# Three score products for a tile instead of four in a chunked gated recurrence (HGRN2) on one core

## The chip, the cores and the metric

The kernel runs on one core of one Trainium2 chip. A core has a matrix engine (PE, with a weight load, PEld, that can run beside the matmuls), a vector engine (DVE), a scalar engine (ACT), a general engine (POOL) and DMA queues, which the kernel issues from SP for the most part. The metric is the device time of one execution in microseconds (us); lower is better. Several executions are timed and the median is given.

## The reference

One layer of a hybrid trunk is computed: adaLN, an HGRN2 gated linear recurrence in both directions over 2048 latent tokens with a prefix of 256 context tokens, an output product, then a gated ConvFFN and a last RMSNorm. The change lies in the recurrence. For each of 8 heads and each direction, with a decay f per token and per key channel, k = 1 - f, and b the running sum of log f:

```python
def hgrn2_chunk_scan(q, k, v, logf, s0):
    """S_t = diag(f_t) S_{t-1} + k_t v_t^T, o_t = S_t^T q_t, in chunkwise form."""
    b = jnp.cumsum(logf, axis=3)
    b_ref = b[:, :, :, CHUNK // 2:CHUNK // 2 + 1]
    b_last = b[:, :, :, -1:]
    qe = q * jnp.exp(b - b_ref)
    ke = k * jnp.exp(b_ref - b)
    scores = jnp.einsum('bhnik,bhnjk->bhnij', qe, ke)
    scores = jnp.where(mask, scores, 0.0)          # causal
    o_intra = jnp.einsum('bhnij,bhnjv->bhniv', scores, v)
    kv = jnp.einsum('bhnjk,bhnjv->bhnkv', k * jnp.exp(b_last - b), v)
    ...                                            # the state S is carried from chunk to chunk
    o_inter = jnp.einsum('bhnik,bhnkv->bhniv', q * jnp.exp(b), s_start)
    o = o_intra + o_inter
```

So a pair (query i, key j) of one chunk has the score q_i . k_j weighted in every channel by the product of the decays between j and i. The forward direction takes j up to i, the backward direction j from i on, and the outputs of both are added.

## The kernel before

**Tiles and units.** The 18 tiles of 128 tokens (two of context, 16 of latents) are taken in two groups of three "units" of three tiles (`GROUPS`). For each group, the loop goes over the 8 heads, and for each head over the three units: 48 calls of `unit`, of which the 8 with the context have one latent tile and 40 have three, so 128 latent tiles times heads in all. A tile of 128 tokens is cut into four segments of 32; a unit has 12 segments (`NS`).

**What a unit does.** Products with the weights go through `mm3` (lines 358 to 360: three fp32r products stand for one of fp32). `unit` first makes the decays of two directions (`d` 0 is the backward one here and `d` 1 the forward one, whose tokens are read in reverse order, line 390), then q and the values v. On DVE it scans the decays within each segment (`S`, line 436, from the segment's far side; then over `F` in the other direction, line 449), forms the keys `ke` (lines 441, 442), the reciprocals `rt` of each segment's total decay (line 451) and the queries `qp` (lines 455, 456). POOL makes from the segment totals the small tables `TB` (decays before and after a segment within its tile) and `TX` (lines 464 to 475). The helper `scaled` (line 480) multiplies a whole operand by one factor per segment: it makes `kd` (keys for the state), `qe` (queries times `rt`), `qi` (queries for the state), and `qm` and `km` (queries and keys for pairs whose segments lie in different halves of the tile). ACT copies `kx`, keys of alternating directions (lines 505, 506).

**What a tile does.** Each tile has a `part_a` and a `part_b`, returned as a list and run during the next unit, between that unit's products (`fill` hands them out). `part_a` transposes `kd` on PE (line 530, evicted by ACT at 532), and makes four products into one PSUM tile `sc` (lines 538, 539, 544, 545): own segment backward, own segment forward, neighbour segment within a half, and across the halves. ACT copies two 64x64 blocks of the fourth (lines 549, 550), DVE copies three more under masks `mx`, `mb`, `mf` (lines 551 to 553) and adds the two halves `af` and `ab` into the score tile `at` (line 554). `part_b` makes the state increment `kv` (line 562), the outputs `o` from the state `Sf` and from `at` (lines 577, 578), evicts them and updates `Sf` (line 581). What the pass over the other direction needs is stored in `stash`.

**What sets the order.** The order in which each engine gets its instructions is not the order of the text: a planner places them by the dependencies between tiles and its own estimate of their times. Tiles of one tag share a fixed number of buffers (`kd` one, `ke`, `qp`, `kx`, `sc` two). After the recurrence come the output product and the ConvFFN, which the change does not touch.

Of the kernel before, what the change touches and what calls it, by code (L numbers as in the profile page):

```python
# [9 lines left out]
F32 = mybir.dt.float32  # L10
F32R = mybir.dt.float32r
BF16 = mybir.dt.bfloat16
U32 = mybir.dt.uint32
# [9 lines left out]
NH = 8  # L23
# [25 lines left out]
def body(ctx, tc, a, out):  # L49
# [123 lines left out]
    def load_feat(h, **kw):  # L173


        feat = []
        for ty in (2, 1):
            wh = wp.tile([128, KT, 128], F32R, name="wh", tag="wh")
            wl = wp.tile([128, KT, 128], F32R, name="wl", tag="wl")
            load_w(h, ty, wh, wl, **kw)  # L180
            feat.append((wh, wl))
        vh = wp.tile([128, KT, 384], F32R, name="vh", tag="vh", bufs=1)
        vl = wp.tile([128, KT, 384], F32R, name="vl", tag="vl", bufs=1)
        load_w(h, 0, vh[:, :, 256:], vl[:, :, 256:], **kw)
        return feat, vh, vl
# [101 lines left out]
    def mixer_scan():  # L287
# [13 lines left out]
        def mask(name):  # L301
            m = fix.tile([128, 4, 32], F32, name=name)
            pool.memset(m, 1.0)
            return m

        mf, mb, mx = mask("mf"), mask("mb"), mask("mx")
        in_block(mb, 32)
        in_block(mx.rearrange("p (a c) b -> p a (c b)", c=2), 64)
        dve.tensor_tensor(mx, mx, mb, OP.subtract)
        in_block(mf, 32)  # L310
        for m, s in ((mf, 1), (mb, -1)):
# [3 lines left out]
        mfu, mbu, mxu = [m.rearrange("p a b -> p (a b)").bitcast(U32) for m in (mf, mb, mx)]  # L315
        d1 = fix.tile([128, NS, SEG], BF16, name="d1")
# [5 lines left out]
        TBs = [fix.tile([128, 4, NSC, 4], F32, name=f"TB{i}") for i in range(2)]  # L322
        TXs = [fix.tile([128, 2, NSC, 4], F32, name=f"TX{i}") for i in range(2)]
        for i in range(2):
            pool.memset(Fs[i], 1.0)
            pool.memset(TBs[i], 1.0)
            pool.memset(TXs[i], 1.0)
            for d in range(2):
                pool.memset(ABs[i][d], 0.0)
# [32 lines left out]
        def unit(h, w, u, tiles, todo):  # L362
# [23 lines left out]
            for d in range(2):  # L386
                z = ps.tile([128, UN], F32, name="z", tag="pj", bufs=3)
                mm3(z, *feat[d], vh, vl)
                zv = z.rearrange("p (c t) -> p c t", t=32)
                act.activation(F[:, d, :, 1:SEG], zv[:, :, 31::-1] if d else zv, AF.Sigmoid)  # L390
                j = (1 - d) * NH + h
                dve.tensor_scalar(F[:, d, :, 1:SEG], F[:, d, :, 1:SEG],
                                  oml[:, j:j + 1], lb[:, j:j + 1], OP.mult, OP.add)
                fill(1 + d)
# [40 lines left out]
            for d in range(2):  # L435
# [4 lines left out]
            ke = gp.tile([128, 2, NS, 32], F32, name="ke", tag="ke", bufs=2)  # L440
            dve.tensor_tensor(ke[:, 0], S[:, 0, :, 0:32], S[:, 0, :, 1:SEG], OP.subtract)
            dve.tensor_tensor(ke[:, 1, :, 31::-1], S[:, 1, :, 0:32], S[:, 1, :, 1:SEG],
                              OP.subtract)


# [6 lines left out]

            qp = gp.tile([128, 2, NS, 32], F32, name="qp", tag="qp", bufs=2)
            qv = q.rearrange("p (c t) -> p c t", t=32)
            dve.tensor_tensor(qp[:, 0, lat], qv, F[:, 0, lat, 1:SEG], OP.mult)
            dve.tensor_tensor(qp[:, 1, lat], qv, F[:, 1, lat, 32:0:-1], OP.mult)

# [12 lines left out]
            pool.tensor_tensor(suf[:, :, :, 0], suf[:, :, :, 1], tot[:, :, :, 1], OP.mult)  # L470
            pool.tensor_copy(decb[:, h, tiles[s0]:tiles[-1] + 1], sd[:, 0, s0:])
            pool.tensor_copy(TX[:, 0, :, 0], tot[:, 0, :, 1])  # L472
            pool.tensor_copy(TX[:, 0, :, 3], tot[:, 1, :, 2])
            pool.tensor_copy(TX[:, 1, :, 0], tot[:, 1, :, 1])
            pool.tensor_copy(TX[:, 1, :, 3], tot[:, 0, :, 2])

            def scaled(dst, src, w):

                w = w[..., None].to_broadcast(list(w.shape) + [32])
                dve.tensor_tensor(dst, src, w, OP.mult)  # L480
# [6 lines left out]
            kd = gp.tile([128, 2, NS, 32], F32, name="kd", tag="kd")  # L487
            scaled(kd, ke, TBf[:, 0:4:3])


            qe = gp.tile([128, 2, NS, 32], F32, name="qe", tag="qe", bufs=2)
            scaled(qe[:, :, lat], qp[:, :, lat], rt[:, :, lat])
            qi = gp.tile([128, 2, NS, 32], F32, name="qi", tag="qi", bufs=2)
            scaled(qi[:, :, lat], qp[:, :, lat], TBf[:, 1:3, lat])


            qm = gp.tile([128, NSC, 4, 32], F32, name="qm", tag="qm", bufs=2)
            km = gp.tile([128, NSC, 4, 32], F32, name="km", tag="km", bufs=2)
            scaled(qm[:, s0:, 0:2], seg(qp[:, 0])[:, :, 0:2], TX[:, 0, s0:, 0:2])
            scaled(qm[:, s0:, 2:4], seg(qp[:, 1])[:, :, 2:4], TX[:, 0, s0:, 2:4])  # L500
            scaled(km[:, s0:, 0:2], seg(ke[:, 1])[:, :, 0:2], TX[:, 1, s0:, 0:2])
            scaled(km[:, s0:, 2:4], seg(ke[:, 0])[:, :, 2:4], TX[:, 1, s0:, 2:4])

            kx = gp.tile([128, NS, 32], F32, name="kx", tag="kx", bufs=2)
            act.activation(kx[:, g0::2], ke[:, 1, g0::2], AF.Copy)
            act.activation(kx[:, g0 + 1::2], ke[:, 0, g0 + 1::2], AF.Copy)

# [18 lines left out]
            def part_a(s):  # L526
# [7 lines left out]
                if s < s0:  # L534
                    return

                sc = ps.tile([128, 4, 128], F32, name="sc", tag="sc", bufs=2)
                pe.matmul(sc[:, 0], ke[:, 0, g4], qe[:, 0, g4], start=True, stop=True)
                pe.matmul(sc[:, 1], ke[:, 1, g4], qe[:, 1, g4], start=True, stop=True)

                c0 = qp[:, 0, 4 * s]
                qx = bass.AP(tensor=c0.tensor, offset=c0.offset,
                             ap=[list(c0.ap[0]), [64, 2], [(NS + 1) * 32, 2], [1, 32]])
                pe.matmul(sc[:, 2], kx[:, g4], qx, start=True, stop=True)
                pe.matmul(sc[:, 3], km[:, s], qm[:, s], start=True, stop=True)
# [4 lines left out]
                act.activation(af[64:128, 0:64], sc[64:128, 3, 0:64], AF.Copy)  # L550
                dve.copy_predicated(af, mxu, sc[:, 2])
                dve.copy_predicated(af, mbu, sc[:, 0])
                dve.copy_predicated(ab, mfu, sc[:, 1])
                dve.tensor_tensor(at, af, ab, OP.add)
                ats[s] = at

            def part_b(s):
# [5 lines left out]
                if s < s0:  # L563
                    kb = gp.tile([128, 3, 128], F32, name="kb", tag="st", bufs=4)
                    act.activation(kb[:, 0], kv[:, 0], AF.Copy)
                    kvb.append(kb[:, 0])
                    if s == 0:
                        dve.tensor_copy(Sf[:, h], kv[:, 1])
                    else:
                        dve.scalar_tensor_tensor(Sf[:, h], Sf[:, h], sd[:, 1, s:s + 1], kv[:, 1],  # L570
                                                 OP.mult, OP.add)
                        dve.scalar_tensor_tensor(Sb[:, h], kvb[1], sd[:, 0, 0:1], kvb[0],
                                                 OP.mult, OP.add)
                    return
                st = sts[s]
                o = ps.tile([128, 128], F32, name="o", tag="o")
                pe.matmul(o, qi[:, 1, g4], Sf[:, h], start=True, stop=False)
                pe.matmul(o, ats[s], v[:, s], start=False, stop=True)
                act.activation(st[:, 0], o, AF.Copy)
                act.activation(st[:, 2], kv[:, 0], AF.Copy)  # L580
                dve.scalar_tensor_tensor(Sf[:, h], Sf[:, h], sd[:, 1, s:s + 1], kv[:, 1],
                                         OP.mult, OP.add)
                t = tiles[s]
                if is_late(h, t):
                    pool.tensor_copy(st[:, 3], qi[:, 0, g4].rearrange("p g t -> p (g t)"))
                    return
# [3 lines left out]
                q_.dma_start(stash[t][:, 0, h, 0], st[:, 2])  # L590
                sp.dma_start(stash[t][:, 0, h, 1], qi[:, 0, g4].rearrange("p g t -> p (g t)"))

# [818 lines left out]
```

## Time and profile before

| what | value |
|---|---|
| time before, median of 3 runs | 2908.31 us (2906.58 to 2913.72) |
| profiled execution: span from first to last instruction | 2911.0 us |
| profiled execution: time around the span | not recorded apart from the span |
| PE busy | 2841.6 us (98%) |
| DVE busy | 2120.3 us (73%) |
| ACT busy | 1168.5 us (40%) |
| POOL busy | 588.7 us (20%) |
| the recurrence | from about 80 to 1370 us of the span |
| mean granted clock of PE | 0.990 |

The profile is of one execution; its span is 2.7 us above the median of the three timed runs. A busy time is the union of an engine's instructions: matmuls overlap in the pipeline, so the duration of one matmul is longer than its share of the engine's time, and the distance from one start to the next is what a matmul costs. An fp32 product of 128 columns is recorded as two matmuls (two passes); an fp32r product is recorded as one.

### The profile page before, as it was taken

What the parts mean: (1) busy time and instruction counts of PE and PEld (TensorE: products, weight loads), DVE (VectorE), ACT (ScalarE), POOL (GpSimd) and SP (SyncE); (2) the same over time, 40 slices, a digit from 0 to 9 for tenths busy, and PEclk for the clock granted to TensorE, in tenths of its full rate; (3) what the DMA queues carried; (4) which work ended last, traced back from release to release, by engine and by line L of the source; (5) the groups of instructions that cost most, each with busy time, mean ns of one, the idle gap of its engine ahead of it and who ended that gap; (6) DMA issues with size and microseconds to landing.
All of it is one profiled execution on the core that took longest, in us unless ns stands there. A gap on an engine that the chain in (4) does not pass through costs nothing.

```text
span 2911.0 us, 44065 instructions
## 1 busy us (share of the span) xinstructions
PE 2841.6 (98%) x16192; PEld 2564.3 (88%) x16192; DVE 2120.3 (73%) x3676; ACT 1168.5 (40%) x2496; POOL 588.7 (20%) x1028
## 2 busy tenths in 40 slices
PE   8899999999999999998999799999999999999999
PEld 8899999998999999998888688888888888887887
DVE  1666666667666667667898498888798887677887
ACT  1533333336333333333455444444444444433343
POOL 1111111111111111111111254434443342000001
PEclk9999999999999999999999899999999999999999
DMA  5022222223222222224677722223622224887663
GB/s 217 25 89 79 80 86 84 77 67 107 81 72 79 77 80 89 70 80 140 237 289 291 307 87 87 87 87 110 238 87 87 87 80 129 271 297 246 204 204 119
DMA packets 202913, 386.57 MB, mean 133 GB/s; under 512 B 26693, under 2 KB 117829, under 8 KB 197449
## 3 DMA queue, kind: packets, MB, share of 16 engines
q1 hardware_dynamic: 199960, 375.51, 38.4%
q10 hardware_dynamic: 2736, 8.26, 0.8%
q8 instruction: 127, 2.08, 0.3%
q14 instruction: 90, 0.73, 0.1%
HBM read 281.70 MB, written 101.99 MB: 132 GB/s over the span
## 4 chain that ended last, share of the span: by engine, by line
PE 90%; DVE 3%; DMA 2%; ACT 2%; issue 1%; POOL 1%; SPq 0%; DVEq 0%; POOLq 0%; ACTq 0%
PE z L360 10%; PE z L359 10%; PE z L358 10%; PE y L1245 4%; PE y L1243 4%; PE y L1244 4%; PE zd L720 3%; PE zc L720 3%; PE zc L722 3%; PE zd L722 3%; PE zd L723 3%; PE zc L723 3%; PE za L720 3%; PE za L722 3%; PE za L723 3%; PE y L804 2%
## 5 line engine op out<-in xcount | busy, mean ns | idle before, releaser
L358 PE MATMUL z<-vh,hh 128*128 128x256 f32 (+1 forms) x1024 | 300.0, 293 | 0.0
L360 PE MATMUL z<-vh,hl 128*128 128x256 f32 (+1 forms) x1024 | 293.5, 287 | 0.0
L359 PE MATMUL z<-vl,hh 128*128 128x256 f32 (+1 forms) x1024 | 293.4, 287 | 0.0
L358 PE MATMUL z<-hh,wh 128*128 128x384 f32 x768 | 263.7, 344 | 9.6 <-ACT hh L80 9.6
L359 PE MATMUL z<-hl,wh 128*128 128x384 f32 x768 | 259.8, 338 | 0.6 <-DVE hl L81 0.5
L360 PE MATMUL z<-hh,wl 128*128 128x384 f32 x768 | 259.8, 338 | 0.0
L1245 PE MATMUL y<-wd,ml 128*128 128x512 f32 x600 | 234.5, 391 | 2.2 <-DVE ml L81 2.1
L1243 PE MATMUL y<-wd,mh 128*128 128x512 f32 x600 | 234.3, 390 | 1.8 <-ACT X L1278 1.8
L1244 PE MATMUL y<-wd,mh 128*128 128x512 f32 x600 | 234.0, 390 | 0.0
L358 PEld LDWEIGHTS z<-vh,hh 128*128 128x128 f32 x1024 | 196.4, 192 | 0.0
L359 PEld LDWEIGHTS z<-vl,hh 128*128 128x128 f32 x1024 | 196.2, 192 | 0.0
L360 PEld LDWEIGHTS z<-vh,hl 128*128 128x128 f32 x1024 | 195.8, 191 | 0.0
L81 DVE TENSOR_TENSOR w<-s,w 128x512 fp32r<-128x512 f32 x132 | 145.6, 1110 | 50.8 <-ACT w L80 50.5
L472 POOL COPY TX<-S 128x3 f32<-128x3 f32 x48 | 15.8, 330 | 775.2 <-DVE S L436 775.2
L81 DVE TENSOR_TENSOR w<-raw,w 128x512 fp32r<-128x512 f32 x176 | 132.2, 754 | 40.2 <-ACT w L80 39.6
L358 PEld LDWEIGHTS z<-hh,wh 128*128 128x128 f32 x768 | 145.6, 190 | 13.6 <-ACT hh L80 10.1
L412 DVE TENSOR_TENSOR st<-z,st 128x128 f32<-128x128 f32 x127 | 36.6, 288 | 157.4 <-ACT st L411 157.3
L1007 DVE SCALAR_TENSOR_TENSOR r<-uv,conv,r 128x1023 f32<-128x1023 f32 (+1 forms) x88 | 150.5, 1728 | 0.4
L80 ACT ACTIVATE w<-raw 128x512 fp32r<-128x512 f32 x176 | 109.0, 627 | 103.3 <-DMA raw<-in_w_up_dram 34.6
L359 PEld LDWEIGHTS z<-hl,wh 128*128 128x128 f32 x768 | 145.8, 190 | 1.3 <-DVE hl L81 1.3
L407 ACT ACTIVATE v<-z 128x128 f32<-128x128 f32 x128 | 35.4, 277 | 275.1 <-PE z L360 275.0
L360 PEld LDWEIGHTS z<-hh,wl 128*128 128x128 f32 x768 | 145.5, 189 | 0.0
(323 smaller groups left out, 8246.8 us busy)
## 6 DMA issues: line engine op xcount, KB each, us to landing
raw<-in_w_up_dram SPq DMA_DIRECT2D x90, 512.0 KB, 3.4
raw<-in_w_in_dram SPq DMA_DIRECT2D x80, 512.0 KB, 3.4
lr<-m SPq DMA_DIRECT2D x49, 512.0 KB, 5.6
m<-r SPq DMA_DIRECT2D x66, 256.0 KB, 3.3
raw<-in_w_ada_dram SPq DMA_DIRECT2D x32, 512.0 KB, 4.5
stash<-st SPq DMA_DIRECT2D x125, 128.0 KB, 1.9
kq<-stash SPq DMA_DIRECT2D x15, 1024.0 KB, 7.4
og<-stash SPq DMA_DIRECT2D x15, 1024.0 KB, 6.9
```

Of the source, the lines that this page charges most:

```text
L80: act.activation(h, src, AF.Copy)
L81: dve.tensor_tensor(l, src, h.bitcast(F32), OP.subtract)
L358: pe.matmul(o, sh[:, k], mh[:, k], start=k == 0, stop=False)
L359: pe.matmul(o, sh[:, k], ml[:, k], start=False, stop=False)
L360: pe.matmul(o, sl[:, k], mh[:, k], start=False, stop=k == KT - 1)
L720: pe.matmul(o, w[:, 0, k], r[:, :, 0, k], start=start and k == 0, stop=False, skip_group_check=True)
L722: pe.matmul(o, w[:, 0, k], r[:, :, 1, k], start=False, stop=False, skip_group_check=True)
L723: pe.matmul(o, w[:, 1, k], r[:, :, 0, k], start=False, stop=k == 3, skip_group_check=True)
L1007: dve.scalar_tensor_tensor(r, x, cw, r, OP.mult, OP.add)
L1243: pe.matmul(z, lh, rh, start=start, stop=False, skip_group_check=True)
L1244: pe.matmul(z, lh, rl, start=False, stop=False, skip_group_check=True)
L1245: pe.matmul(z, ll, rh, start=False, stop=stop, skip_group_check=True)
```

## The change

Keys and queries get different weights from before, so that three products hold all pairs of a tile. Direction 0 becomes the forward one and direction 1 the backward one. For segments taken alternately, either the keys or the queries are multiplied in place by `rt`: the keys `ke` of odd segments in direction 0 and of even segments in direction 1, and the queries `qp` of the other parity. The separate operands `qe`, `qm` and `km` are gone. A third plane of `qp`, called `far`, holds the queries for the other half of the tile. The first product takes `kx` against the scaled queries, the second and third take `ke` of one direction against unscaled queries of alternate segments and `far`. Their PSUM tile has three parts instead of four. Two masks and two masked copies take the place of three; the second goes to two blocks of columns at once. `kx` is copied by one ACT instruction instead of two. `TX` has one table instead of two, made by two copies and two products instead of four copies. The masks are built once, at the start, by another list of POOL instructions.

```diff
-        for ty in (2, 1):
+        for ty in (1, 2):
...
-        mf, mb, mx = mask("mf"), mask("mb"), mask("mx")
...
+        mx, my, mw = mask("mx"), mask("my"), mask("mw")
+        in_block(mx, 32)
+        pool.tensor_copy(mw, mx)
+        causal(mx, False)
+        causal(mw, True)
+        pool.tensor_copy(mx[:, 1::2], mw[:, 1::2])
+        pool.memset(mw, 1.0)
+        in_block(mw.rearrange("p (a c) b -> p a (c b)", c=2), 64)
+        pool.tensor_copy(by_two(my)[:, 0], by_two(mw)[:, 0])
+        pool.tensor_copy(by_two(my)[:, 1], by_two(mw)[:, 1])
...
-                act.activation(F[:, d, :, 1:SEG], zv[:, :, 31::-1] if d else zv, AF.Sigmoid)
-                j = (1 - d) * NH + h
+                act.activation(F[:, d, :, 1:SEG], zv if d else zv[:, :, 31::-1], AF.Sigmoid)
+                j = d * NH + h
...
-            qp = gp.tile([128, 2, NS, 32], F32, name="qp", tag="qp", bufs=2)
+            qp = gp.tile([128, 3, NS, 32], F32, name="qp", tag="qp", bufs=2)
...
-            pool.tensor_copy(TX[:, 0, :, 0], tot[:, 0, :, 1])
-            pool.tensor_copy(TX[:, 0, :, 3], tot[:, 1, :, 2])
-            pool.tensor_copy(TX[:, 1, :, 0], tot[:, 1, :, 1])
-            pool.tensor_copy(TX[:, 1, :, 3], tot[:, 0, :, 2])
+            pool.tensor_copy(TX[:, :, 1], tot[:, 0, :, 1])
+            pool.tensor_copy(TX[:, :, 2], tot[:, 1, :, 2])
+            pool.tensor_tensor(TX[:, :, 0], tot[:, 1, :, 1], tot[:, 1, :, 2], OP.mult)
+            pool.tensor_tensor(TX[:, :, 3], tot[:, 0, :, 1], tot[:, 0, :, 2], OP.mult)
...
-            scaled(kd, ke, TBf[:, 0:4:3])
-            qe = gp.tile([128, 2, NS, 32], F32, name="qe", tag="qe", bufs=2)
-            scaled(qe[:, :, lat], qp[:, :, lat], rt[:, :, lat])
+            scaled(kd, ke, TBf[:, 1:3])
             qi = gp.tile([128, 2, NS, 32], F32, name="qi", tag="qi", bufs=2)
-            scaled(qi[:, :, lat], qp[:, :, lat], TBf[:, 1:3, lat])
-            qm = gp.tile([128, NSC, 4, 32], F32, name="qm", tag="qm", bufs=2)
-            km = gp.tile([128, NSC, 4, 32], F32, name="km", tag="km", bufs=2)
-            scaled(qm[:, s0:, 0:2], seg(qp[:, 0])[:, :, 0:2], TX[:, 0, s0:, 0:2])
-            scaled(qm[:, s0:, 2:4], seg(qp[:, 1])[:, :, 2:4], TX[:, 0, s0:, 2:4])
-            scaled(km[:, s0:, 0:2], seg(ke[:, 1])[:, :, 0:2], TX[:, 1, s0:, 0:2])
-            scaled(km[:, s0:, 2:4], seg(ke[:, 0])[:, :, 2:4], TX[:, 1, s0:, 2:4])
+            scaled(qi[:, :, lat], qp[:, 0:2, lat], TBf[:, 0:4:3, lat])
+            far = seg(qp[:, 2])
+            scaled(far[:, :, 0::2], seg(qp[:, 1])[:, :, 0:2], TX[:, s0:, 0::2])
+            scaled(far[:, :, 1::2], seg(qp[:, 0])[:, :, 2:4], TX[:, s0:, 1::2])
+            def walk(x, *ap):
+                return bass.AP(tensor=x.tensor, offset=x.offset, ap=[list(x.ap[0]), *ap])
+            def every_other(x, n, odd):
+                return walk(x[:, 0, g0 + odd], [(NS + 1 - 2 * odd) * n, 2],
+                             [2 * n, (NS - g0) // 2], [1, n])
             kx = gp.tile([128, NS, 32], F32, name="kx", tag="kx", bufs=2)
-            act.activation(kx[:, g0::2], ke[:, 1, g0::2], AF.Copy)
-            act.activation(kx[:, g0 + 1::2], ke[:, 0, g0 + 1::2], AF.Copy)
+            act.activation(kx[:, g0:].rearrange("p (a c) t -> p c a t", c=2),
+                           every_other(ke, 32, 0), AF.Copy)
+            for x, odd in ((ke, 1), (qp, 0)):
+                w = every_other(rt[..., None], 1, odd).to_broadcast([128, 2, (NS - g0) // 2, 32])
+                x = every_other(x, 32, odd)
+                dve.tensor_tensor(x, x, w, OP.mult)
...
-                sc = ps.tile([128, 4, 128], F32, name="sc", tag="sc", bufs=2)
-                pe.matmul(sc[:, 0], ke[:, 0, g4], qe[:, 0, g4], start=True, stop=True)
-                pe.matmul(sc[:, 1], ke[:, 1, g4], qe[:, 1, g4], start=True, stop=True)
...
-                pe.matmul(sc[:, 2], kx[:, g4], qx, start=True, stop=True)
-                pe.matmul(sc[:, 3], km[:, s], qm[:, s], start=True, stop=True)
+                sc = ps.tile([128, 3, 128], F32, name="sc", tag="sc", bufs=2)
+                zig = [[64, 2], [(NS + 1) * 32, 2], [1, 32]]
+                pe.matmul(sc[:, 0], kx[:, g4], walk(qp[:, 0, 4 * s], *zig), start=True, stop=True)
+                for d in (1, 0):
+                    qx = walk(qp[:, d, 4 * s + 1 - d], [(2 - d) * NS * 32, 2], [64, 2], [1, 32])
+                    pe.matmul(sc[:, 2 - d], ke[:, d, g4], qx, start=True, stop=True)
...
-                act.activation(af[0:64, 64:128], sc[0:64, 3, 64:128], AF.Copy)
-                act.activation(af[64:128, 0:64], sc[64:128, 3, 0:64], AF.Copy)
-                dve.copy_predicated(af, mxu, sc[:, 2])
-                dve.copy_predicated(af, mbu, sc[:, 0])
-                dve.copy_predicated(ab, mfu, sc[:, 1])
+                act.activation(af[64:128, 0:64], sc[64:128, 1, 64:128], AF.Copy)
+                act.activation(af[0:64, 64:128], sc[0:64, 2, 64:128], AF.Copy)
+                dve.copy_predicated(ab, mxu, sc[:, 0])
+                dve.copy_predicated(by_two(af.rearrange("p (a b) -> p a b", b=32)), myu,
+                                    sc[:, 1:3, 0:64].rearrange("p c (a b) -> p c a b", b=32))
                 dve.tensor_tensor(at, af, ab, OP.add)
```

In `part_b` the indices of the two directions are exchanged to match, and nothing else.

More of the change, by code (lines that the diff above doesn't have):

```diff
@@ L304, in mask, with causal, by_two @@
             return m
-        mf, mb, mx = mask("mf"), mask("mb"), mask("mx")
[L307 to L311, printed above, removed]
+        def causal(m, back):
+            s = -1 if back else 1
             pool.affine_select(out=m, in_=m, pattern=[[32 * s, 4], [s, 32]],
                                compare_op=OP.is_ge, fill=0.0, base=0, channel_multiplier=-s)
-        mfu, mbu, mxu = [m.rearrange("p a b -> p (a b)").bitcast(U32) for m in (mf, mb, mx)]
+        def by_two(m):
+            return m.rearrange("p (a c) b -> p c a b", c=2)
+        mx, my, mw = mask("mx"), mask("my"), mask("mw")
[8 more added lines that the diff above has]
+        pool.tensor_copy(by_two(my)[:, 1], by_two(mw)[:, 1])
+        pool.affine_select(out=my[:, 0::2], in_=my[:, 0::2], pattern=[[-64, 2], [-1, 32]],
+                           compare_op=OP.is_ge, fill=0.0, base=0, channel_multiplier=1)
+        pool.affine_select(out=my[:, 1::2], in_=my[:, 1::2], pattern=[[64, 2], [1, 32]],
+                           compare_op=OP.is_ge, fill=0.0, base=32, channel_multiplier=-1)
+        mxu = mx.rearrange("p a b -> p (a b)").bitcast(U32)
+        myu = by_two(my).bitcast(U32)
         d1 = fix.tile([128, NS, SEG], BF16, name="d1")
@@ L322, in mixer_scan @@
         TBs = [fix.tile([128, 4, NSC, 4], F32, name=f"TB{i}") for i in range(2)]
-        TXs = [fix.tile([128, 2, NSC, 4], F32, name=f"TX{i}") for i in range(2)]
+        TXs = [fix.tile([128, NSC, 4], F32, name=f"TX{i}") for i in range(2)]
         for i in range(2):
@@ L326, in mixer_scan @@
             pool.memset(TBs[i], 1.0)
-            pool.memset(TXs[i], 1.0)
             for d in range(2):
@@ L440, in unit @@
             ke = gp.tile([128, 2, NS, 32], F32, name="ke", tag="ke", bufs=2)
-            dve.tensor_tensor(ke[:, 0], S[:, 0, :, 0:32], S[:, 0, :, 1:SEG], OP.subtract)
-            dve.tensor_tensor(ke[:, 1, :, 31::-1], S[:, 1, :, 0:32], S[:, 1, :, 1:SEG],
+            dve.tensor_tensor(ke[:, 0, :, 31::-1], S[:, 0, :, 0:32], S[:, 0, :, 1:SEG],
                               OP.subtract)
+            dve.tensor_tensor(ke[:, 1], S[:, 1, :, 0:32], S[:, 1, :, 1:SEG], OP.subtract)
             for d in range(2):
@@ L451, in unit @@
             dve.reciprocal(rt[:, :, lat], S[:, :, lat, 32])
-            qp = gp.tile([128, 2, NS, 32], F32, name="qp", tag="qp", bufs=2)
+            qp = gp.tile([128, 3, NS, 32], F32, name="qp", tag="qp", bufs=2)
             qv = q.rearrange("p (c t) -> p c t", t=32)
-            dve.tensor_tensor(qp[:, 0, lat], qv, F[:, 0, lat, 1:SEG], OP.mult)
-            dve.tensor_tensor(qp[:, 1, lat], qv, F[:, 1, lat, 32:0:-1], OP.mult)
+            dve.tensor_tensor(qp[:, 0, lat], qv, F[:, 0, lat, 32:0:-1], OP.mult)
+            dve.tensor_tensor(qp[:, 1, lat], qv, F[:, 1, lat, 1:SEG], OP.mult)
             tot = S[:, :, :, 32].rearrange("p d (s g) -> p d s g", g=4)
@@ L470, in unit @@
             pool.tensor_tensor(suf[:, :, :, 0], suf[:, :, :, 1], tot[:, :, :, 1], OP.mult)
-            pool.tensor_copy(decb[:, h, tiles[s0]:tiles[-1] + 1], sd[:, 0, s0:])
-            pool.tensor_copy(TX[:, 0, :, 0], tot[:, 0, :, 1])
-            pool.tensor_copy(TX[:, 0, :, 3], tot[:, 1, :, 2])
-            pool.tensor_copy(TX[:, 1, :, 0], tot[:, 1, :, 1])
-            pool.tensor_copy(TX[:, 1, :, 3], tot[:, 0, :, 2])
+            pool.tensor_copy(decb[:, h, tiles[s0]:tiles[-1] + 1], sd[:, 1, s0:])
+            pool.tensor_copy(TX[:, :, 1], tot[:, 0, :, 1])
+            pool.tensor_copy(TX[:, :, 2], tot[:, 1, :, 2])
+            pool.tensor_tensor(TX[:, :, 0], tot[:, 1, :, 1], tot[:, 1, :, 2], OP.mult)
+            pool.tensor_tensor(TX[:, :, 3], tot[:, 0, :, 1], tot[:, 0, :, 2], OP.mult)
             def scaled(dst, src, w):
@@ L535, in part_a @@
                     return
-                sc = ps.tile([128, 4, 128], F32, name="sc", tag="sc", bufs=2)
[L538 to L545, printed above, removed]
+                sc = ps.tile([128, 3, 128], F32, name="sc", tag="sc", bufs=2)
[4 more added lines that the diff above has]
+                    pe.matmul(sc[:, 2 - d], ke[:, d, g4], qx, start=True, stop=True)
                 at = gp.tile([128, 128], F32, name="at", tag="at", bufs=2)
@@ L564, in part_b @@
                     kb = gp.tile([128, 3, 128], F32, name="kb", tag="st", bufs=4)
-                    act.activation(kb[:, 0], kv[:, 0], AF.Copy)
+                    act.activation(kb[:, 0], kv[:, 1], AF.Copy)
                     kvb.append(kb[:, 0])
                     if s == 0:
-                        dve.tensor_copy(Sf[:, h], kv[:, 1])
+                        dve.tensor_copy(Sf[:, h], kv[:, 0])
                     else:
-                        dve.scalar_tensor_tensor(Sf[:, h], Sf[:, h], sd[:, 1, s:s + 1], kv[:, 1],
+                        dve.scalar_tensor_tensor(Sf[:, h], Sf[:, h], sd[:, 0, s:s + 1], kv[:, 0],
                                                  OP.mult, OP.add)
-                        dve.scalar_tensor_tensor(Sb[:, h], kvb[1], sd[:, 0, 0:1], kvb[0],
+                        dve.scalar_tensor_tensor(Sb[:, h], kvb[1], sd[:, 1, 0:1], kvb[0],
                                                  OP.mult, OP.add)
@@ L576, in part_b @@
                 o = ps.tile([128, 128], F32, name="o", tag="o")
-                pe.matmul(o, qi[:, 1, g4], Sf[:, h], start=True, stop=False)
+                pe.matmul(o, qi[:, 0, g4], Sf[:, h], start=True, stop=False)
                 pe.matmul(o, ats[s], v[:, s], start=False, stop=True)
                 act.activation(st[:, 0], o, AF.Copy)
-                act.activation(st[:, 2], kv[:, 0], AF.Copy)
-                dve.scalar_tensor_tensor(Sf[:, h], Sf[:, h], sd[:, 1, s:s + 1], kv[:, 1],
+                act.activation(st[:, 2], kv[:, 1], AF.Copy)
+                dve.scalar_tensor_tensor(Sf[:, h], Sf[:, h], sd[:, 0, s:s + 1], kv[:, 0],
                                          OP.mult, OP.add)
@@ L584, in part_b @@
                 if is_late(h, t):
-                    pool.tensor_copy(st[:, 3], qi[:, 0, g4].rearrange("p g t -> p (g t)"))
+                    pool.tensor_copy(st[:, 3], qi[:, 1, g4].rearrange("p g t -> p (g t)"))
                     return
@@ L590, in part_b @@
                 q_.dma_start(stash[t][:, 0, h, 0], st[:, 2])
-                sp.dma_start(stash[t][:, 0, h, 1], qi[:, 0, g4].rearrange("p g t -> p (g t)"))
+                sp.dma_start(stash[t][:, 0, h, 1], qi[:, 1, g4].rearrange("p g t -> p (g t)"))
             order = ((part_a, 0), (part_a, 1), (part_b, 0), (part_a, 2), (part_b, 1), (part_b, 2))
```

## The prediction

> **What bounds the kernel now.** I read the page first: busy shares and the chain that ended last.
>
> ```profile
> span 2911.0 us, 44065 instructions
> ...
> PE 2841.6 (98%) x16192; PEld 2564.3 (88%) x16192; DVE 2120.3 (73%) x3676; ACT 1168.5 (40%) x2496; POOL 588.7 (20%) x1028
> ...
> PE 90%; DVE 3%; DMA 2%; ACT 2%; issue 1%; POOL 1%; SPq 0%; DVEq 0%; POOLq 0%; ACTq 0%
> ```
>
> PE is busy nearly everywhere and carries 90% of the chain. These are averages, though, and the change touches only the recurrence, so next I cut that stage into stretches, once for all instructions (columns: stretch and its length, then busy us and count of PE, PEld, DVE, ACT, POOL, then granted clock, DMA share, GB/s) and once for those that write or read the score tile `sc` alone (no POOL column).
>
> ```profile
> 60.00:150.00 90.00, 73.29 (x444) 69.00 (x443) 62.34 (x139) 48.61 (x112) 13.07 (x32) 0.98 0.08 26
> 150.00:645.00 495.00, 494.49 (x3498) 487.80 (x3497) 323.55 (x734) 167.69 (x516) 78.76 (x251) 1.00 0.26 80
> 645.00:745.00 100.00, 92.56 (x653) 89.05 (x652) 72.21 (x166) 62.90 (x147) 15.87 (x44) 0.97 0.29 95
> 745.00:1344.00 599.00, 598.38 (x4338) 592.34 (x4337) 397.08 (x872) 200.06 (x613) 78.84 (x254) 1.00 0.26 80
> 1344.00:1370.00 26.00, 23.89 (x185) 22.68 (x183) 19.12 (x44) 10.51 (x35) 4.06 (x12) 1.00 0.43 139
> ```
>
> ```profile
> 60.00:150.00 90.00, 4.96 (x32) 4.12 (x32) 2.98 (x12) 1.72 (x8) 0.98 0.08 26
> 150.00:645.00 495.00, 47.55 (x360) 43.70 (x360) 35.15 (x135) 19.52 (x90) 1.00 0.26 80
> 645.00:745.00 100.00, 9.78 (x72) 9.23 (x72) 7.16 (x27) 3.87 (x18) 0.97 0.29 95
> 745.00:1344.00 599.00, 69.74 (x528) 64.10 (x528) 51.34 (x199) 28.64 (x132) 1.00 0.26 80
> 1344.00:1370.00 26.00, 4.33 (x32) 3.88 (x32) 3.06 (x12) 1.73 (x8) 1.00 0.43 139
> ```
>
> In 150 to 645 and 745 to 1344 PE has 494.49 of 495 us and 598.38 of 599 us: no gap to speak of, at full clock, while DVE works 65% and 66% of the time. A tile has eight passes of `sc` on PE (four products, two passes each), so the counts give 4, 45, 9, 66 and 4 tiles: 128 in all, and 45 + 66 = 111 of them lie where PE is the bound beyond doubt. The other 17 lie where PE idles 16.7, 7.4 and 2.1 us. Last I listed whom PE waits for in the recurrence and what the queues of DVE and ACT wait for (total us, times, longest).
>
> ```profile
> PE tp L112 <- ACT xt L103: 7.2, 7, 3.3
> PE sc L538 <- DVE qe L480: 0.3, 1, 0.3
> ACT F L390 <- PE z L360: 144.4, 61, 5.4
> ACT kx L505 <- DVE ke L442: 72.3, 45, 3.0
> DVE kd L480 <- PE tr L530: 21.8, 17, 2.3
> ```
>
> PE waited for the score operands once, 0.3 us. So an operation taken from PE is worth its place in PE's stream.
>
> **The product removed.** A matmul's duration overlaps its neighbours, so I take the distance between starts, in the list of PE in order of time (start, length):
>
> ```profile
> 800.30 0.39 PE L538 MATMUL sc<-qe,ke 128*128 128x128 f32 x2
> 800.52 0.39 PE L539 MATMUL sc<-qe,ke 128*128 128x128 f32 x2
> 800.75 0.39 PE L544 MATMUL sc<-qp,kx 128*128 128x128 f32 x2
> 800.97 0.39 PE L545 MATMUL sc<-qm,km 128*128 128x128 f32 x2
> 801.19 0.61 PE L562 MATMUL kv<-v,kt 128*128 128x128 f32 x4
> ```
>
> Four products from 800.30 to 801.19 are 0.89 us, 0.2225 us each, 0.111 us a pass. (The union of `sc` in 745 to 1344, 69.74 us for 264 products, is 0.264 each; it holds the overlap at each group's end and is the upper bound.) 128 products x 0.2225 = 28.5 us; only the 111 certain tiles: 24.7 us; by the union: 33.8 us. I take 28.5: in the three looser stretches PE is still busy 81% to 93% of the time, so most of the other 3.8 us comes back too.
>
> [...]
>
> **The work on DVE, ACT and POOL.** From the groups by line, shapes kept apart (busy us, mean ns):
>
> ```profile
> L480 DVE TENSOR_TENSOR qe<-qp,rt 128x768 f32<-128x768 f32 x40 | 38.1, 952 | 0.0
> L480 DVE TENSOR_TENSOR qm<-qp,TX 128x192 f32<-128x192 f32 x80 | 28.1, 352 | 0.0
> L480 DVE TENSOR_TENSOR km<-ke,TX 128x192 f32<-128x192 f32 x80 | 26.9, 337 | 3.2 <-POOL TX L474 2.6
> L455 DVE TENSOR_TENSOR qp<-q,F 128x384 f32<-128x384 f32 x40 | 22.1, 552 | 0.0
> L551 DVE COPY_PREDICATED AB<-mx,sc 128x128 f32<-128x128 uint32 x128 | 37.0, 291 | 3.3 <-ACT AB L550 3.3
> L505 ACT ACTIVATE kx<-ke 128x192 f32<-128x192 f32 x40 | 14.6, 365 | 67.5 <-DVE ke L442 67.5
> L390 ACT ACTIVATE F<-z 128x384 f32<-128x384 f32 x96 | 46.7, 487 | 144.7 <-PE z L360 144.4
> L475 POOL COPY TX<-S 128x3 f32<-128x3 f32 x48 | 22.8, 475 | 0.0
> ```
>
> DVE, for each of the 40 full units: `qe` 0.952, two `qm` 0.704 and two `km` 0.674 go, 2.33 us; two for `far` (0.704, the shape of `qm`) and two in-place products of 384 elements (1.104, the shape of L455) come, 1.81 us: 0.52 x 40 = 21 us less. For each tile one masked copy of 0.291 goes: 37 us less. The copy to two blocks keeps 128 columns but has broken rows; its form is not in the trace. I take 0.291; if it costs twice that, the 37 us are gone and DVE's total is still below before's. An in-place product could cost from 0.352 (half its elements) to 0.952 (twice): between 16 us less and 32 us more over 80 of them. So DVE changes by +11 us at the worst, -74 at the best with the copy at 0.291, and -58 as I take it. ACT: two copies of 365 ns become one of 384 elements, about 487, 0.24 x 40 = 10 us less, and at the ends 0 to 15 less. All of this is worth nothing in itself: DVE has 202 idle us in 745 to 1344 alone. With that cover gone, each microsecond more on DVE would be one on the path.
>
> POOL: four table copies become two and two products of three elements; nothing either way, and at the dearest row here, 475 ns, POOL's queue grows by less than a microsecond a unit. Masks: some more POOL instructions, once, in the first 15 us, before the recurrence starts at about 80; their cover is POOL's long wait just before it, 51 us by this row of POOL's list in order of time:
>
> ```profile
> 78.86 0.55 POOL L77 TENSOR_TENSOR rs<-rs,mhalf 128x1 f32<-128x1 f32 x1 [51.17 <-DVE rs L76]
> ```
>  The exchange of the directions and the order of the two weight loads moves equal work in equal shapes; no DMA is added, and none on SP's queue or POOL's moves past another, beyond two weight loads of 512 KB that trade places.
>
> **New waits.** The in-place product on `ke` must follow `kd` (which reads the unscaled keys, on the same engine) and ACT's `kx` copy. So DVE now waits for ACT there, with `qp`'s scaling, the values' products and the next masked copies behind it; and `kd`, with one buffer, waits in turn for PE's transposes. All three products now need the last of that chain; before, `qm` was last:
>
> ```profile
> 807.14 0.35 DVE L480 TENSOR_TENSOR qm<-qp,TX 128x192 f32<-128x192 f32 x1
> ...
> 816.00 0.39 PE L538 MATMUL sc<-qe,ke 128*128 128x128 f32 x2
> ```
>
> The last operand was ready at 807.49 and PE used it at 816.00: 8.5 us to spare, because `part_a` runs in the next unit. `kx` waits for `ke`, not `ke` for `kx`: ACT is early at that point, and the longest hold of ACT's queue, 5.4 us, is inside the 8.5. I cost the new waits at 0; at their worst, one 5.4 us hold that still falls short of the 8.5 gives 0, and in the first stretch, with less room, perhaps 2 us.
>
> Sum: 2911.0 - 28.5 = 2882.5 us for the profiled execution; it stands 2.7 us above the median of 2908.3, so the median becomes 2879.8. I say 2880.
>
> **The rivals.**
>
> (1) Part of the product comes back as waits in the loose stretches. For it: PE idles there for ACT's `xt` and the `hm` chain, so a freed 0.22 us may only lengthen that. Against: just 17 tiles. 24.7 us less, 2883.6. Or a pass taken out returns less than its distance, because work of its neighbours fills the place; at three quarters of 0.111, 21 us less, 2887. With a few new waits besides, up to 2893.
>
> (2) More than the product: DVE's lighter load also shortens the waits of PE in those stretches (26 us idle in sum). If a fifth of it goes, 33.7 us less: 2874.6. Against: the largest of them, `xt`, is set by ACT and POOL.
>
> (3) No change within 0.3% (8.7 us, about what a measurement of this kernel can tell): PE's freed time is all spent waiting, 0.15 us a tile or more. For it: three products instead of two now hang on one late chain. Against: the 8.5 us. 2900 to 2917.
>
> (4) Slower: DVE held by ACT at the in-place product on `ke`. When it passes the 8.5 us of room, PE stalls and its clock falls too. That is seen after the one long wait in this trace:
>
> ```profile
> 709.21 1.12 PE L112 MATMUL tp<-ident,xt 128*128 128x128 f32 x4 [3.33 <-ACT xt L103]
> ...
> 709.80:713.40 3.60, 3.60 (x14) 3.60 (x13) 1.37 (x4) 0.00 (x0) 0.00 (x0) 0.50 0.00 0
> ```
>
> After 3.33 us of waiting, 3.6 us went at a granted clock of 0.50, 1.8 us lost: 5.1 us a stall. To be slower by 0.3% takes 28.5 + 8.7 = 37.2 us, eight such stalls, or one in six units: 2879.8 + 8 x 5.1 = 2920.6 us. [...] Against: no hold of ACT in the list reaches 8.5 us.
>
> **How the numbers follow.** Forecast (25 to 31 us less, 2877 to 2883): 0.62. Rival 2, 2871 to 2877: 0.12. Rival 1 beyond the forecast, 2883 to 2900: 0.18. Rival 3: 0.05. Rival 4: 0.03. Faster is 0.62 + 0.12 + 0.18 = 0.92. The range 2872 to 2893 takes in the forecast, nearly all of rival 2 and most of rival 1 (both ends of the product's price, 24.7 and 33.8, lie in it): about 0.85.
>
> **What would show it.** The page after should have 256 PE instructions fewer, PE's busy time lower by about 28 us, and the recurrence's end, at about 1370 before, some 28 us earlier, with the stages behind it as long as before. The starts of three products and what follows should stand 0.22 us apart. DVE's busy time should fall by some 58 us; the two-block copy and the in-place products show their own durations. PE's list of waits should have no `sc` row beyond 2 us, and DVE's no large row for ACT's `kx`. The prediction is wrong if the two PE-bound stretches show gaps or a clock under 1.00, if the passes left stand wider apart, or if the planner's new order starves PE elsewhere.

## The result and the profile after

The changed kernel takes 2879.3 us (median of four runs, 2876.2 to 2880.5) against 2910.4 before (2906.6 to 2913.7): a ratio of 0.989, interval 0.9875 to 0.9906, about 31 us less. The forecast was 2880.

The page of the changed kernel (span; busy us of each engine):

```profile
span 2874.5 us, 43322 instructions
...
PE 2808.6 (98%) x15936; PEld 2530.5 (88%) x15936; DVE 2061.7 (72%) x3499; ACT 1158.0 (40%) x2448; POOL 606.0 (21%) x1031
```

PE has 256 instructions and 33.0 us less, DVE 58.6 us less, ACT 10.5 less; POOL has 17.3 us more.

To see where the time came from I used marks that stand at the same place of the work in every kernel: PE's products with the vector of ones in the adaLN rows (`z<-acc`, line 616 before), four pairs of them in the recurrence. They cut out two stretches that lie wholly where PE is the bound, the first with 20 tiles and the third with 24. Before, then after (stretch and length, busy us and count of PE, PEld, DVE, ACT, POOL, clock, DMA share, GB/s):

```profile
356.50:554.90 198.40, 198.40 (x1407) 195.64 (x1407) 131.88 (x300) 68.76 (x211) 29.80 (x96) 1.00 0.27 84
1002.10:1221.80 219.70, 219.70 (x1590) 217.07 (x1589) 146.18 (x321) 73.49 (x225) 29.39 (x96) 1.00 0.28 85
```

```profile
354.60:548.40 193.80, 193.80 (x1367) 191.01 (x1367) 124.32 (x272) 66.98 (x203) 31.20 (x96) 1.00 0.28 86
982.20:1196.30 214.10, 214.10 (x1542) 211.51 (x1542) 136.96 (x289) 71.53 (x217) 30.76 (x96) 1.00 0.29 87
```

PE is busy for the whole of each stretch, before and after. Their sum goes from 418.1 to 407.9 us, 10.2 us for 44 tiles, 0.232 us a tile. The stretch between them, which also has 44 tiles and in which the group of tokens changes and PE idles, goes from 447.2 to 433.8, 13.4 us. All in all the profiled spans differ by 36.5 us: 29.3 by the start of the recurrence's last product, 1.9 more in the wait for the stash behind it, and 5.3 in the stages after it, which the change does not touch. From the start of PE's first `oi` product to the span's end, where all kernels of this document do the same work, the thirteen profiled executions took 1527.5 to 1535.4 us, before being the longest. So I take the 5.3 us as the scatter of single executions, and the medians' 31 as the better number.

The changed groups, with line, shapes, busy us, mean ns, idle time before:

```profile
L563 PE MATMUL sc<-qp,ke 128*128 128x128 f32 x512 | 79.1, 275 | 0.0
L560 PE MATMUL sc<-qp,kx 128*128 128x128 f32 x256 | 49.5, 275 | 0.0
L570 DVE COPY_PREDICATED AB<-my,sc 128x128 f32<-128x128 uint32 x128 | 37.8, 295 | 0.0
L527 DVE TENSOR_TENSOR qp<-qp,rt 128x384 f32<-128x384 f32 x40 | 22.0, 550 | 0.1
L527 DVE TENSOR_TENSOR ke<-ke,rt 128x384 f32<-128x384 f32 x40 | 22.0, 549 | 0.0
L522 ACT ACTIVATE kx<-ke 128x384 f32<-128x384 f32 x40 | 21.0, 526 | 74.8 <-DVE ke L457 74.8
L486 POOL COPY TX<-S 128x3 f32<-128x3 f32 x48 | 29.9, 623 | 760.9 <-DVE S L450 760.9
```

The last column, the idle time of the engine just before these instructions, is what matters for the new waits: PE never waited ahead of `sc`, and DVE (0.1 us in all) hardly ahead of the in-place products, neither for ACT's `kx` nor for anything else.

### The profile page after: what moved, and what is told of

Read it like the earlier page. It is cut to its first block, busy times and chain, and to the rows that moved or that the text cites. A ratio compares the mean times of both kernels' runs of the same rounds, so it can differ in the third digit from the quotient of the medians.

```text
span 2874.5 us, 43322 instructions
## 1 busy us (share of the span) xinstructions
PE 2808.6 (98%) x15936; PEld 2530.5 (88%) x15936; DVE 2061.7 (72%) x3499; ACT 1158.0 (40%) x2448; POOL 606.0 (21%) x1031
## 4 chain that ended last, share of the span: by engine, by line
PE 81%; DVE 7%; DMA 6%; ACT 2%; issue 2%; POOL 1%; SPq 0%; DVEq 0%; POOLq 0%; ACTq 0%
PE z L372 10%; PE z L374 10%; PE z L373 10%; PE zd L740 3%; PE zd L738 3%; PE zd L741 3%; PE zc L740 3%; PE zc L738 3%; PE zc L741 3%; PE za L740 3%; PE za L738 3%; PE za L741 3%; PE y L1263 3%; PE y L1261 3%; PE y L1262 3%; PE kv L580 2%
## 5 line engine op out<-in xcount | busy, mean ns | idle before, releaser
L372 PE MATMUL z<-hh,wh 128*128 128x384 f32 x768 | 264.5, 345 | 10.2 <-ACT hh L80 10.2
L486 POOL COPY TX<-S 128x3 f32<-128x3 f32 x48 | 29.9, 623 | 760.9 <-DVE S L450 760.9
```

Source lines behind the costliest of these rows:

```text
L372: pe.matmul(o, sh[:, k], mh[:, k], start=k == 0, stop=False)
```

## The experiments

All are compared in the two bound stretches, by the sums over both (418.1 before, 407.9 after), and by medians against the runs of before in their own series. The runs were made in three series, whose medians of before were 2906.6, 2906.1 and 2907.1 us; where a kernel is set against one of another series, the text says so. The diffs show the lines that matter and leave out what was adapted to them.

**A fourth product put back.**

```diff
+                pe.matmul(sc[:, 3], ke[:, 0, g4], walk(qp[:, 0, 4 * s], *zig), start=True, stop=True)
```

> The changed kernel with a fourth product for each tile put back on PE, with the operands ke and the scaled qp; its result is read by nobody, and DVE, ACT and POOL keep the changed kernel's lighter work. Theory (PE's passes are the price): all of the gain goes, 28.5 us over the changed kernel, within 3 us of the time before. Rival (DVE's lighter work is the gain): the time stays that of the changed kernel, within 5 us.

> The changed kernel as it is, for a closer time. Theory (256 passes of PE, 0.111 us each, in a stage that PE bounds): 28.5 us under before, and whatever the later stages add or take, so 27 to 32 us. Rival (the chain of the recurrence was held by DVE, whose work also fell by about 59 us): no other time is expected of this run, it is the point the next ones are measured from.

2901.8 us against 2876.4 for the changed kernel in the same series: 25.4 us back, 3 less than forecast, and still 4.8 below before where 3 were allowed (against before: 0.9988, interval 0.9979 to 0.9998). What is left over is taken up below. The bound stretches, summed:

```profile
sum 418.10, PE 418.10 PEld 412.72 DVE 262.13 ACT 138.49 POOL 62.93; mean PE 209.05 PEld 206.36 DVE 131.06 ACT 69.24 POOL 31.46
```

This is exactly before's 418.1, although DVE has 262.1 us of work in it instead of 278.1. The rival, that DVE's lighter work is the gain, predicted no change and is out.

**One product less in the kernel before.**

```diff
-                pe.matmul(sc[:, 3], km[:, s], qm[:, s], start=True, stop=True)
...
-                act.activation(af[0:64, 64:128], sc[0:64, 3, 64:128], AF.Copy)
+                act.activation(af[0:64, 64:128], sc[0:64, 2, 64:128], AF.Copy)
...
```

> The kernel before with the fourth product (across the halves) left out of each tile and the two ACT copies reading the third product's part in its place; the scores across the halves are wrong by that. DVE's work is as before. Theory: 28.5 us faster than before, the changed kernel's time. Rival (DVE): no faster than before by more than 5 us.

2875.0 against 2906.6 (0.9896, 0.988 to 0.9912), the changed kernel's time:

```profile
sum 407.50, PE 407.50 PEld 402.20 DVE 276.69 ACT 142.25 POOL 63.52; mean PE 203.75 PEld 201.10 DVE 138.35 ACT 71.12 POOL 31.76
```

Taking out the product alone, with DVE's work as before, gives 31.6 us by the medians, as much as the whole change (30.3 in this series).

**DVE's work less, all four products kept.**

```diff
-            scaled(qe[:, :, lat], qp[:, :, lat], rt[:, :, lat])
-            scaled(qm[:, s0:, 0:2], seg(qp[:, 0])[:, :, 0:2], TX[:, 0, s0:, 0:2])
...
-                dve.copy_predicated(af, mbu, sc[:, 0])
```

> The kernel before with all four products, but with the scalings for qe, qm and km and one masked copy left out (the products take the unscaled queries and keys), so that DVE has about 2.33 x 40 + 37 = 130 us less to do, twice and more what the change took from it. Theory: no change, within 4 us of before, or a few us faster from the stretches in which PE is not the bound. Rival (DVE): at least the change's whole gain, 28 us or more.

2905.1 against 2906.6 (0.9996, 0.9987 to 1.0005): no change that can be told. DVE's busy time fell by 103 us (2120.3 to 2017.2), not by 130: the durations that were added up overlap on DVE too (in before's list `qe` at 805.40 has 0.95 us, and the next operation starts 0.87 us after it).

```profile
sum 418.10, PE 418.10 PEld 412.68 DVE 244.07 ACT 143.22 POOL 62.17; mean PE 209.05 PEld 206.34 DVE 122.03 ACT 71.61 POOL 31.09
```

34 us of DVE's work are gone from these stretches, and not 0.1 us of time.

**Two products and five.**

```diff
-                pe.matmul(sc[:, 0], kx[:, g4], walk(qp[:, 0, 4 * s], *zig), start=True, stop=True)
-                dve.copy_predicated(ab, mxu, sc[:, 0])
+                dve.copy_predicated(ab, mxu, kt[:, 0])
```

That was for two products; for five:

```diff
+                for d in (0, 1):
+                    pe.matmul(sc[:, 3], ke[:, d, g4], walk(qp[:, 0, 4 * s], *zig), start=True, stop=True)
```

> The changed kernel with the first of its three products left out (the own-segment scores it holds are replaced by other numbers of the same shape), everything else as it is. Theory (each product of 128 columns costs its place in PE's stream, whichever it is): 25 to 29 us under the changed kernel, by the 25 us that a fourth product added and the 31 us that taking one from the kernel before gave. Rival (three products were already at the point where another engine or the weight products bound the stage): less than 10 us under it.

> The changed kernel with two further products for each tile whose results nobody reads, five in all. Theory: twice the price of one, 51 to 57 us over the changed kernel, so 20 to 27 us over the time before. Rival (the price of one more product grows or shrinks with their number, by waits that come or go): outside 45 to 63 us over the changed kernel.

> The changed kernel as it is, in one series with the two others, as the point between them: 28 to 31 us under before.

In this series two, three and five products took 2855.4, 2877.2 and 2926.1 us (against before 0.9815, 0.9799 to 0.9831; 0.9897, 0.9882 to 0.9913; 1.0064, 1.0051 to 1.0078). With 2901.8 for four, from the series before, one product is worth 21.8, 24.6 and 24.3 us: near to even, and a little below what was expected (25 to 29 for the product taken out, 51 to 57 for the two added, which cost 48.9). Neither rival shows: there is no knee down to two. The sums for two and for five:

```profile
sum 398.80, PE 398.79 PEld 393.13 DVE 260.86 ACT 136.52 POOL 68.81; mean PE 199.39 PEld 196.57 DVE 130.43 ACT 68.26 POOL 34.40
```

```profile
sum 426.90, PE 426.90 PEld 421.80 DVE 264.76 ACT 137.70 POOL 69.96; mean PE 213.45 PEld 210.90 DVE 132.38 ACT 68.85 POOL 34.98
```

398.8, 407.9, 418.1, 426.9: steps of 9.1, 10.2 and 8.8 us over 44 tiles, 0.21, 0.23 and 0.20 us a product.

**What a pass is made of: half the columns, and twice.**

```diff
-                    pe.matmul(sc[:, 2 - d], ke[:, d, g4], qx, start=True, stop=True)
+                    pe.matmul(sc[:, 2 - d, 0:64], ke[:, d, g4], walk(qp[:, d, 4 * s + 1 - d], [64, 2], [1, 32]),
+                              start=True, stop=True)
```

```diff
-                pe.matmul(sc[:, 0], kx[:, g4], walk(qp[:, 0, 4 * s], *zig), start=True, stop=True)
+                pe.matmul(sc[:, 0:2], kx[:, g4], walk(qp[:, 0, 4 * s], [NS * 32, 2], [1, 128]), start=True, stop=True)
```

> The changed kernel with the second and third product narrowed from 128 moving columns to the 64 of the near segments; the scores across the halves are left out (ACT copies other numbers of the same shape into their place). The weights loaded stay 128x128. Theory A, a product's price is its moving columns: half of two products goes, 0.111 x 2 x 128 = 28 us under the changed kernel. Theory B, its price is the weight load (which stays): no gain over the changed kernel, within 3 us. If both weigh the same, a little under A's end or B's end tells which is the longer.

> The changed kernel with the first product widened from 128 to 256 moving columns under the same weights; the further columns are read by nobody in their old meaning, and what is read for the first product is wrong in part of the segments. Theory A, moving columns: 28.5 us over the changed kernel, the time before. Theory B, weight loads: within 3 us of the changed kernel.

Narrow: 2873.0 us, 0.9891 of before (0.9875 to 0.9908), the changed kernel's ratio. Wide: 2900.5, 0.9982 (0.9973 to 0.9991), nearly back at before. The sums, narrow and then wide:

```profile
sum 407.30, PE 407.30 PEld 402.15 DVE 259.97 ACT 142.25 POOL 65.04; mean PE 203.65 PEld 201.08 DVE 129.99 ACT 71.13 POOL 32.52
```

```profile
sum 417.10, PE 417.10 PEld 409.47 DVE 262.02 ACT 138.48 POOL 62.97; mean PE 208.55 PEld 204.74 DVE 131.01 ACT 69.24 POOL 31.48
```

Halving the columns of two products saved 0.6 us of the 10 that half of two products would be; doubling those of one cost 9.2 us. PE's list in order of time shows how (narrow first, then its weight loads, then wide):

```profile
780.16 0.56 PE L563 MATMUL sc<-qp,ke 128*128 128x64 f32 x4
780.55 0.66 PE L581 MATMUL kv<-v,kt 128*128 128x128 f32 x4
781.05 0.39 PE L596 MATMUL o<-Sf,qi 128*128 128x128 f32 x2
```

```profile
780.05 0.53 PEld L563 LDWEIGHTS sc<-qp,ke 128*128 128x128 f32 x4
780.50 0.53 PEld L581 LDWEIGHTS kv<-v,kt 128*128 128x128 f32 x4
780.95 0.30 PEld L596 LDWEIGHTS o<-Sf,qi 128*128 128x128 f32 x2
```

```profile
789.58 0.60 PE L560 MATMUL sc<-qp,kx 128*128 128x256 f32 x2
790.02 0.61 PE L563 MATMUL sc<-qp,ke 128*128 128x128 f32 x4
790.46 0.61 PE L580 MATMUL kv<-v,kt 128*128 128x128 f32 x4
```

Four passes of 64 columns still take 0.39 us, and the four of `kv` behind them 0.50 instead of the 0.44 that four passes of 128 columns take in the last fence: 0.89 for eight, as with 128 columns. The weight loads stand 0.11 us apart, four in 0.45 us, beside the narrow passes as beside the full ones. Two passes of 256 columns take 0.44 us, double. So theory B fits the 64 columns (0.11 us a pass, those behind them counted in) and theory A the 256 (0.22 us): the three widths fit a pass that costs the longer of its weight load, 0.11 us here, and its columns, 0.11 for 128. No run changed the size of the weights, so that it is their load which holds the narrow pass, and not another fixed cost of a pass, is read from the list of loads and not shown by a run.

**How much cover DVE leaves.**

```diff
+            for _ in range(2):
+                scaled(jk[:, :, lat], qi[:, :, lat], TBf[:, 0:4:3, lat])
+                scaled(qi[:, :, lat], jk[:, :, lat], TBf[:, 0:4:3, lat])
```

> The changed kernel with four more DVE products of 768 elements in each full unit, chained ahead of the far queries and the scalings in place (3.8 us a unit, about 155 us of DVE in all; the queries for the state are wrong by that). Theory (DVE is covered, 8.5 us to spare): no change, within 5 us of the changed kernel. Rival (the three products hang on a late DVE chain): each microsecond shows, up to 150 us more, and PE's waits name sc.

> As the last, with ten products of 768 elements (9.5 us a unit, about 385 us of DVE in all). In the steady stretch DVE has about 213 us idle of 595, 8.9 us for each of 24 units, so here the cover should be gone: theory 25 to 120 us over the changed kernel, with PE waiting for DVE in each unit. If it is still within 5 us, the room is larger than read from the trace.

The run with ten has `range(5)`. Four more: 2885.5 us (0.9933, 0.9919 to 0.9948), 9 us over the changed kernel of the first series, where 5 were allowed. Ten more: 2910.1 (1.0011, 1.0002 to 1.0021), 34 us over, within what was expected but not for the reason given: PE did not wait for DVE in each unit. The sums for four and ten:

```profile
sum 407.70, PE 407.70 PEld 402.38 DVE 309.56 ACT 138.65 POOL 62.92; mean PE 203.85 PEld 201.19 DVE 154.78 ACT 69.32 POOL 31.46
```

```profile
sum 408.40, PE 408.01 PEld 402.49 DVE 382.86 ACT 138.73 POOL 83.62; mean PE 204.00 PEld 201.24 DVE 191.43 ACT 69.36 POOL 41.81
```

In the bound stretches DVE can go from 261 to 383 of 408 us, 94%, and costs 0.5 us. The loss lies in the loose stretches. With four more, the stretch of the group change took 442.0 us between the marks, where three executions of the changed kernel took 433.6 to 436.2; the piece after the last mark grew by 1 us, the others not beyond their scatter. In the stretch of the group change PE idled 12.7 us instead of 6.5 to 6.8. With ten more, the pieces up to the first mark, across the group change and after the last mark grew by 6, 15 and 13 us against the first execution of the changed kernel, and in the last PE waited once for `qi` (total us, times, longest):

```profile
PE o L599 <- DVE qi L494: 8.7, 1, 8.7
```

The added products did not lengthen the chain that the score products wait for as the text of the kernel has it. DVE's list in order of time, with ten, and PE's next use of the scaled queries:

```profile
836.25 0.95 DVE L494 TENSOR_TENSOR jk<-qi,TB 128x768 f32<-128x768 f32 x1
837.12 0.55 DVE L531 TENSOR_TENSOR ke<-ke,rt 128x384 f32<-128x384 f32 x1
837.59 0.95 DVE L494 TENSOR_TENSOR qi<-jk,TB 128x768 f32<-128x768 f32 x1
838.46 0.55 DVE L531 TENSOR_TENSOR qp<-qp,rt 128x384 f32<-128x384 f32 x1
838.93 0.95 DVE L494 TENSOR_TENSOR jk<-qi,TB 128x768 f32<-128x768 f32 x1
```

```profile
846.92 0.39 PE L564 MATMUL sc<-qp,kx 128*128 128x128 f32 x2
```

The planner put both scalings in place behind two of the ten products, here and in 40 of the 48 units, and the other eight after them. From the end of the scaling of `qp` to the unit's first score product there are 9.2 us in the changed kernel (median of the 48 units) and 7.4 with four or ten more. So that chain came 1.8 us later, not 3.8 or 9.5, and PE's waits name `sc` with 2.2 us in all (four) and 2.1 (ten). What came much later is `qi`, the queries for the state: its room before PE's use fell from 16.6 to 4.3 us (medians, ten more). The runs show that a DVE filled to 94% is covered in the bound stretches; what a score chain later than its room would cost is not shown.

## Why the prediction was right, point by point

**The product removed** (28.5 us, taken at 0.2225 us each). Its place in PE's stream was the price: 0.232 us a tile in the bound stretches, 0.20 to 0.23 over the other steps. But over the whole kernel a product between three and four was worth only 25.4 us. Where these lie can be read from the start of each tile's first score product, the tiles counted in PE's order and cut into the five stretches of the prediction (4, 45, 9, 66 and 4 tiles). The table has the time in us by which the first kernel took longer than the second in each; the first column has the three executions of the changed kernel in turn, the second the first of them.

| stretch | product put back against changed | before against changed | before against product put back |
|---|---|---|---|
| up to the first bound tile | -1.2, -1.7, 0.8 | -2.3 | -1.1 |
| 45 bound tiles | 10.5, 10.4, 10.4 | 10.4 | -0.1 |
| 9 tiles, group change | 0.6, -1.8, 0.8 | 5.3 | 4.7 |
| 66 bound tiles | 15.0, 15.0, 15.0 | 15.1 | 0.1 |
| last 4 tiles, up to the first `oi` | 0.6, 0.4, 0.6 | 2.7 | 2.1 |

The 111 bound tiles return 25.4 to 25.5 us in every pair, 0.23 each. For the other 17 the three executions give -0.1, -3.1 and 2.3 us, nothing that can be told from the scatter of single executions. So the step "most of the other 3.8 us comes back too" does not show: it is rival 1's sum of 24.7, with 0.23 instead of 0.2225 a tile, that the product met. Rival 1's three quarters of 0.111 us a pass is shown by no run: over the kernel a product added or taken out under the new code was worth 22 to 25 us, and the steps in the bound stretches give 0.100 to 0.116 us a pass.

**The rest of the gain.** From 25.4 to the 30 or 31 of the medians 5 us are left, and the difference between before and the kernel with a product put back is just resolved: 0.6 to 6.1 us by its interval. It is not in the bound stretches (418.1 and 418.1). In the profiles of the recurrence it is for the most part in the stretch of the group change, 447.2 for before, 442.5 for four products under the new code. There PE waits for `xt`, the next group's tokens that ACT scales for PE's transposes `tp`; before, and with four products under the new code, in 600 to 800 us (total us, times, longest):

```profile
PE tp L112 <- ACT xt L103: 6.7, 6, 3.3
```

```profile
PE tp L112 <- ACT xt L103: 4.6, 6, 2.0
```

PE idles 7.5 us of this stretch in before and 5.4 with the product put back: 2.0 us of the difference. The other 2.7 fit the clock. After its wait of 3.3 us before ran on at a granted clock of 0.50; in the 6.8 us of it PE was busy for 5.49, and half of these, 2.7, are an estimate of the loss. With the product put back the longest wait was 2.0 us, and the clock stayed at 1.00 (first before, then the same place with the product put back):

```profile
707.90:714.70 6.80, 5.49 (x20) 5.40 (x21) 1.66 (x5) 1.64 (x2) 0.07 (x1) 0.50 0.00 0
```

```profile
700.00:715.00 15.00, 13.00 (x94) 12.42 (x92) 10.95 (x22) 9.57 (x24) 4.82 (x13) 1.00 0.42 130
```

The prediction cut its window for this stall too short, 709.80 to 713.40: by this estimate it cost 3.33 + 2.74 = 6.1 us, not 5.1. It had counted the stall only as a risk, in rival 4, not as something that the change could remove.

So rival 2's place was right and its cause was not: with 103 us less on DVE and the old code, this stretch took 446.6, with a wait of 3.4 us and a granted clock of 0.94 in 690 to 720 us. The old code with one product less had no wait over 1.5 us there and took 433.2, about as long as the changed kernel (433.8). So taking the product out of the old code returned 26.0 us in the 111 bound tiles, and the long wait and the lower clock were gone besides (1.00 in 690 to 720 us, against 0.89 in before). Why the waits for `xt` are longer in some of these programs than in others is not shown. The planner's order of the instructions around them is the likely reason; no run changed the order alone. The clock behind a wait differed even between two executions of one program, as the last section shows.

The forecast of 28.5 us thus met 30 to 31 (31.1, 30.3 and 29.9 in three series) because a loss of some 3 us on the product and a gain of some 5 beside it nearly cancel. The mechanism and the price of a pass were right; that the sum came out so close was luck.

**DVE, ACT and POOL.** Costed at nothing. For DVE the kernel with less work on it shows that to hold (103 us less, 0.9996 of before); no run changed the work of ACT or POOL alone. Most sizes held too: the two-block copy at 295 ns for 291, the in-place products at 550 for 552, ACT -10.5 for -10, although `kx` took 526 ns, not 487. POOL grew by 17.3 us, 0.36 a unit, below the microsecond allowed. On DVE the -58.6 us of the page are close to the -58 by luck: up to the first `oi` product DVE's busy time fell from 881.0 to 830.1 us, 51 less, and the rest is in stages that the change does not touch.

**New waits.** Costed at 0; there were none ahead of `sc` or of the in-place products. The 8.5 us of room for the late chain, read from one unit, fits: the median over the units is 9.2 us, before and after. In the bound stretches no run used it up, since the added products moved that chain by 1.8 us only. In the loose stretches 3.8 us more of DVE a unit cost 9 us in all. That is far from a microsecond for each microsecond, as the prediction had it for a DVE without cover: 146 us more of DVE cost 9.

## What to carry to other kernels

Where the profile showed PE busy for the whole of a stretch, a product taken from it was worth about the distance between its starts there (0.23 us a tile, for 0.2225 in the list); in the stretches with gaps nothing could be told from the scatter (the 17 loose tiles, -3.1 to 2.3 us). Work taken from DVE at 66% was worth nothing (34 us less of it, 418.1 us with and without), and even at 94% DVE was covered to 0.5 us of 408, with a consumer that ran a unit behind. When an experiment adds work to a chain, look in the trace whether the work stands in that chain: here a planner had moved most of it behind. For an fp32 product under 128x128 weights, narrowing the moving operand from 128 to 64 columns gained next to nothing (0.6 us of 407.9, where a whole product less gave 9.1): what saved here was to drop the product, not its columns.

## What the runs showed of the hardware that was not expected

The same program was granted different clocks after the same wait. Two executions of the changed kernel have a wait of PE of 2.8 us at the group change (start, length, instruction, wait); the first kept the clock and the second did not:

```profile
699.43 0.66 PE L112 MATMUL tp<-ident,xt 128*128 128x128 f32 x4 [2.77 <-ACT xt L103]
```

```profile
699.87 1.12 PE L112 MATMUL tp<-ident,xt 128*128 128x128 f32 x4 [2.80 <-ACT xt L103]
```

```profile
690.00:720.00 30.00, 26.69 (x196) 25.81 (x194) 19.74 (x45) 18.92 (x46) 5.89 (x15) 1.00 0.30 98
```

```profile
690.00:720.00 30.00, 26.96 (x182) 26.19 (x181) 19.64 (x43) 17.38 (x43) 5.34 (x14) 0.89 0.31 99
```

The four transposes took 0.66 or 1.12 us, the products of 384 columns behind them stood 0.17 or 0.32 us apart, the granted clock in those 30 us was 1.00 or 0.89, and the stretch between the marks took 433.8 or 436.1: 2.3 us between two executions of one program, with the same waits to 0.3 us. The length of the wait alone does not decide it in the other runs either. In the run with half the columns a wait of 2.19 us for `xt` was followed, from 1.4 us after its end, by 3.3 us in which the products stood 0.32 us apart. After waits of 2.30 us (256 columns) and 3.11 us (four more on DVE) they stood 0.17 us apart.
